# Gate and up pairs in seven products: two of the four weight sums made by adding DMAs, with signs turned

## The chip, the core and the metric

The kernel runs on one core of one Trainium2 chip, alone. The metric is the time of one execution on the device in microseconds (us). The core has five engines with queues of their own: TensorE (PE in the profile, its weight loads PEld), VectorE (DVE), ScalarE (ACT), GpSimd (POOL) and SyncE (SP). Each works through its instructions in order and waits on semaphores. 16 DMA engines move data between device memory and SBUF; a transfer is begun by a queue of SyncE, ScalarE or GpSimd.

## The reference

One layer of a hybrid decoder: a SwiGLU network, a mixer (gated linear attention beside stick-breaking attention), and a second SwiGLU network, each with RMS norms around it. The change is in the gate and up products of both networks:

```python
def swiglu(x, w_gate, w_up, w_down):
    return (jax.nn.silu(x @ w_gate) * (x @ w_up)) @ w_down

h = x + 0.5 * rms_norm(swiglu(rms_norm(x, ffn1_pre_g), ffn1_w_gate, ffn1_w_up, ffn1_w_down), ffn1_post_g)
# ... the mixer ...
y = h + 0.5 * rms_norm(swiglu(rms_norm(h, ffn2_pre_g), ffn2_w_gate, ffn2_w_up, ffn2_w_down), ffn2_post_g)
```

The model width is 1024, the hidden width 2816 (22 tiles of 128), all in float32. There are 512 prompt tokens, 32 sample tokens and 16 meta tokens: 560 columns in the first network, 544 in the second.

## The kernel before

A float32 product is made of three matmuls: each operand is split into a high part, its rounding to fp32r (`hi`, made by ScalarE), and a low part, the rest (`lo`, made by VectorE), and high times high, low times high and high times low are added up in PSUM.

**Tiles R and S.** Of the 22 hidden tiles of a network, 0 to 2 are computed early by halves of the columns, 3 to 5 (R in `PLAN1` and `PLAN2`) in the plain way, and 6 to 21 (S) in seven products: 16 pairs in each network, 32 in all. A pair is gate and up of one tile. Its activations are taken as a 2 x 2 matrix of quarters (halves of the columns by halves of the 1024 inputs), its weights too (halves of the inputs by gate and up). Seven products of quarters or of sums of quarters, 4 k-steps of 3 matmuls each (`seven`, matmuls in lines 1266 to 1268), give the four output quarters after a few additions. That is 84 matmuls of 280 or 272 columns.

**The weight sums.** A weight quarter is 512 x 128, in SBUF 128 x 512. `Chunks.fetch` loads a pair with two calls, each into one `raw` tile of 128 x 1024 by two DMAs on SyncE's queue (line 638): r1 holds b11 (gate, upper half of the inputs) and b12 (up, upper half), r2 holds b22 (up, lower half) and b21 (gate, lower half). `weight_sums` (line 988) makes four differences on VectorE, each a tensor_tensor of 128 x 512 by the helper `tt` (line 166):

```python
t3 = b22 - b12      # into a tile t
t1 = b12 - b11      # in place, over b12 in r1
t2 = b22 - t1       # into the tile t
t4 = b21 - t2       # into a tile t4
```

`parts_of` then splits r1 (called b1), t, r2 (b2) and t4 into high and low parts (`parted`, line 977, and `parted_lo`). The low part of b1 and of b2 frees the raw tile, and the same step calls `fetch` for the next load. There are three raw tiles, so b2 of a pair frees the tile for r1 of the pair after next.

**The order.** The order on TensorE, VectorE, ScalarE and GpSimd is that in which the code issues it: `step()` is called after every 6 matmuls of a pair, and `weights_at` hangs work on these steps, counted from the pair's first matmul: the four sums at -10, -10, -9 and -8, b1 at -6 and -5 (high part, low part), t at -2 and -1, b2 at 0 and 1, t4 at 4 and 6. A pair has 14 steps. SyncE's queue is ordered by a scheduler.

**The activation sums** (`summed`, line 1134) are made once for each network, four for each of two pairs of k-tiles, by `tt`. **The outputs** are put together on VectorE from PSUM (`add`, `c22`, `c21` and a sum for c12 in `seven`).

**Space.** Nearly all else lies in one arena of SBUF. `PLACES` is a table of bytes that says for each `take` where its tile is put (names room...). An instruction that writes into a place waits for the last readers of what was there.

The down projections and the mixer's gates use `weight_sums` and `parts_of` too.

Of the kernel before, what the change touches and what calls it, by code (L numbers as in the profile page):

```python
# [9 lines left out]
F32 = mybir.dt.float32  # L10
# [4 lines left out]
ALU = mybir.AluOpType  # L15

P = 128
D = 1024
KD = D // P
# [30 lines left out]


PLACES = bytes.fromhex("""
0c060018121e242a7094908082848668766a5066565e5c787c5452724e7a5836221c884c8c6c3064484a6e60613a2e8a3e446236923c465a3036
281674404260917e91588e124e328c341e726c307e4a4c188a486e3e24647a882c3c38360c06625a6a42749244402a3a2e0c00605e5c1e201254
147c16220664465283006268826980660b50560660680a69866467808400620b660a0c2661066460676686186300606266671004650662646766
86286100646066671a10620660878663660c1c00621d8786640e2506662486871c60910064688786241a690666688687820a6800246564697662
6806666991008264690078680607082491770776681c069186424e3e343a74546e7266323c00368c4468767c2840781e6c820c0238708c762a2e
26927c8a040660622a2c4816246527702e1262186071152c622a2b2d6415712c1262632a622a2b2d642c71626306180c1e62714b71246a003254
883e64604b38020434308a6058763c786222122a482e4c4a8e2c7b84668c687e7f406056464f3d333579036b366e747044426c7215015939318b
7782893f055514157a804e5a7e825c2483284e655e92647c508d3a521e148c822667648466616764656766422c7016604668746c6e647244206a  # L60
0a6612088a6c1804343c8c780688916a761a720f026e22320e1c103057565584641486544000760c676a6c8a7248082e604c1a3e582a910e2c66
301c856e001257421002685655542040164675150c8a146a0a300e121e188c782a2c007074107620060421863442736c6e728988846475668e0c
17343e12324c4a42460b7476486a3c1c3004436e20080972621a3736876660860a436c8417686e8e6a642c1488568c430408063c906394708417
6664606c6e78728e8a68846a86606e17708468646a6c7894728e668a0c866e606c176478686a848e728a66706e6c866072177084026836646a6c
8e00786686948a6e401c6620721a1e178a646030948e106c0c6a0e181c2068708486366e786a4072102a221e20170094667038840e1a6e8e0c1c
60724068641c8a1e1a186c220260206e8e59540e2a0c84721e302e68100066606c94641e3840202200706694308e8464606e4740721002682e0e
6c6630002a6884548c880c1456648e6e701660946c586e0c040e463c144754621206329074442e087674582c0a6c160c40102e2c006611466e43
705658544472340862403010322a1200024406343090916e0a436d0610160c72620840909066466c726c625670540a58406e084672020e540a6e
44163c4000100c064614404372561213020410703c3d423e000e4c6e161246483c060444420b1048704c0a023e494072006e480e14166e424412
463c560a2a7460309461704c8c8d2e904a4862766660346c6d670e88303276406c8c6663629500102c623e8876947254586667000e0a01006667  # L70
00105466403e88560d0c7273000c068a508e86202264366a1e7c7880268492524e34603a141a7e487a68734246824a733c3e58901b1717722e38
6e174c2840245a17175c7074442a5e5d1876668c54509212583e903c12151556622c88526c1b484a464215687f7b7e7a151b683a4e601b6a845c
1b18678d8053932d3078156577556381891c2282516d57648a5e1272384c2e1e828e906e868418403e36582416749432426a340c00605a5c484a
30683c44463a0c4e62702a56882c121e922022066416547f00607a7e7b80660b768c0662640a650c6c677e7800640e66060a600f06620e67660c
7a1000641166670e0419066218676610801800641966671a0c1906621c181d660a1b0064241a251c18630666266227241a65001c286429261067
06244e664f280e5000261d1c064e62520624292800501c4f00264e080928062524020308006c14862c486672504c8e4e1268926052880208047a
64304a2e3c82600a5884220c0280566a622410460e1e360842000a060418200302060e10030211060c0d0504020c110304020e1005030c181e30
24363d3440243a3e243865268202906c626e70
""")


class Arena:
# [52 lines left out]
def hybrid_step(  # L135
# [16 lines left out]
    take, give = arena.take, arena.give  # L152
# [6 lines left out]
    count = [0]  # L159
# [5 lines left out]
    def tt(out, a, b, op, eng=None):  # L165
        (eng or V).tensor_tensor(out=out, in0=a, in1=b, op=op)  # L166

    def stt(out, a, s, b, op0, op1):
        V.scalar_tensor_tensor(out=out, in0=a, scalar=s, in1=b, op0=op0, op1=op1)  # L169
# [454 lines left out]
    class Chunks:  # L624
# [5 lines left out]
        def fetch(self):  # L630
            if self.todo:
                w, r0, kt, c0, nw, kept = self.todo.pop(0)
                if kept == "quarters":

                    count[0] += 1
                    raw = sp.tile([P, kt, nw], F32, tag="raw", name=f"raw{count[0]}")
                    for i, w_ in enumerate(w):
                        nc.sync.dma_start(raw[:, 4 * i : 4 * i + 4],
                                          w_[r0 : r0 + 4 * P, c0 : c0 + nw].rearrange("(k p) n -> p k n", p=P))
# [323 lines left out]
    def gate_up_weights(plan, g_, u_, f0):  # L963
        for f in range(f0, KF):
            if f < RE_FFN or plan[f - RE_FFN] == "R":
                st.todo.extend((w, 0, KD, P * f, P, f < RE_FFN and "tile") for w in (g_, u_))
            else:
                st.todo.extend((w, r0, KD, P * f, P, "quarters") for w, r0 in (((g_, u_), 0), ((u_, g_), 4 * P)))

    quarters = {}  # L970

    def parted(f, key, src, room=None):

# [14 lines left out]
    def weight_sums(f, n):  # L988

        if n == 0:  # L990
            quarters[f] = st.raws.pop(0)[0], st.raws.pop(0)[0], take(KD * P), take(4 * P)
        r1, r2, t, t4 = quarters[f]
        t, t4 = (x.rearrange("p (k n) -> p k n", n=P) for x in (t, t4))
        b11, t1, b22, b21, t2, t3 = r1[:, :4], r1[:, 4:], r2[:, :4], r2[:, 4:], t[:, :4], t[:, 4:]
        tt(*((t3, b22, t1), (t1, t1, b11), (t2, b22, t1), (t4, b21, t2))[n], ALU.subtract)

    def parts_of(f, key):
        r1, r2, t, t4 = quarters[f]
# [95 lines left out]
    def other_tiles(old, gain, rs, nw, wid, hid, pairs, plan, late, sums_at, begun):  # L1094
# [5 lines left out]
        QW = nw // 2  # L1100
        QS = (slice(0, QW), slice(QW, nw))
# [4 lines left out]
        start_, n = {}, 0  # L1106
# [27 lines left out]
        def summed(i, n):  # L1134

            x, y = (pairs_of(pr_[j]) for j in (i, i + 2))
            if n == 0:
                for m in range(2):
                    sr_[i, m] = take(2 * NT)
            (s1, s2), (s3, s4) = ([pairs_of(sr_[i, m])[:, :, c] for c in QS] for m in range(2))  # L1140
            a11, a21, a12, a22 = x[:, :, QS[0]], x[:, :, QS[1]], y[:, :, QS[0]], y[:, :, QS[1]]
            tt(*((s1, a21, a22, ALU.add), (s3, a11, a21, ALU.subtract), (s2, s1, a11, ALU.subtract), (s4, a12, s2, ALU.subtract))[n])

        def sums_hi(i, m):
            for k in range(2):
# [75 lines left out]
        def seven(f):  # L1221
# [3 lines left out]
            o = {}  # L1225
# [16 lines left out]

            def c22():
                o["up"], o["sl"] = take(NT), take(NT)
                tt(o["up"][:, QS[1]], o["u2"][:, :QW], o["v"][:, :QW], ALU.add)
                give(o["v"])

            def c21():
# [1501 lines left out]
```

## Time and profile before

| | us |
|---|---|
| three runs | 1492.54, 1493.01, 1493.69 |
| median | 1493.01 |
| span of the profiled execution | 1491.2 |
| TensorE busy in it | 1482.6 |
| VectorE busy | 1106.0 |
| ScalarE busy | 783.1 |
| GpSimd busy | 68.4 |
| packets of queue q1 (SyncE), share of the 16 DMA engines | 44.7% |

The profile is of one execution on the chip. L12 is line 12 of the kernel; most of VectorE's instructions stand at the lines of two helpers, 166 (`tt`) and 169 (`stt`). A row of a group reads: line, engine, operation, output <- inputs by the program's names, sizes in partitions x elements, count | busy us, mean ns of one | idle time of the engine before them and what ended it. A row of the timeline begins with its start and its length in us. SPq is SyncE's queue of DMAs.

### The profile page before, as it was taken

To read this page: it belongs to the slowest core of one execution; us is meant where nothing else is said; L and a number is where in the kernel's file an instruction comes from. 1 tells how busy PE (TensorE), PEld (TensorE's weight loads), DVE (VectorE), ACT (ScalarE), POOL (GpSimd) and SP (SyncE) were. 2 spreads that over 40 slices of the span, in tenths; PEclk is the share of its full clock that TensorE was granted. 3 is DMA by queue.
4 is the path that set the end of the run, shared out by engine and by line. 5 is a ranking of instruction groups with operands and counts; after the bars stand their busy time and mean duration, and the time that the engine had idled before them with its cause. 6 is when DMAs were issued, how large, how long until landed. Compare 5 with 4: busy or idle time off the path is not lost.

```text
span 1491.2 us, 29865 instructions
## 1 busy us (share of the span) xinstructions
PE 1482.6 (99%) x11909; PEld 1435.2 (96%) x11909; DVE 1106.0 (74%) x1945; ACT 783.1 (53%) x1453; POOL 68.4 (5%) x145
## 2 busy tenths in 40 slices
PE   9999999999999999999999999999999999999998
PEld 8999999999999899999998999999999999999998
DVE  5888888855677866877887845777567898888544
ACT  7455454533555656566666543634564455455333
POOL 2000000000000011112111000000000000000000
PEclk9999999999999999999999999999999999999999
DMA  8133333324665584336555866344531333333253
GB/s 253 50 92 100 100 96 92 97 79 123 172 153 138 148 151 100 86 95 161 125 112 160 228 162 200 96 110 140 155 111 52 100 100 100 99 107 92 79 152 115
DMA packets 277230, 181.97 MB, mean 122 GB/s; under 512 B 10429, under 2 KB 255363, under 8 KB 277091
## 3 DMA queue, kind: packets, MB, share of 16 engines
q1 hardware_dynamic: 276786, 180.00, 44.7%
q8 instruction: 93, 1.52, 0.4%
q14 instruction: 47, 0.38, 0.1%
q0 software_dynamic: 288, 0.07, 0.0%
q10 hardware_dynamic: 16, 0.00, 0.0%
HBM read 155.06 MB, written 24.97 MB: 121 GB/s over the span
## 4 chain that ended last, share of the span: by engine, by line
PE 96%; DVE 2%; ACT 1%; DMA 1%; issue 0%; DVEq 0%; ACTq 0%
PE acc L1266 8%; PE acc L1267 8%; PE acc L1268 8%; PE acc L699 7%; PE acc L700 7%; PE acc L702 7%; PE acc L712 6%; PE acc L715 6%; PE acc L713 6%; PE acc L1046 2%; PE acc L1047 2%; PE acc L1048 2%; PE acc L1209 2%; PE acc L1206 2%; PE acc L1207 2%; PE ps L2041 1%
## 5 line engine op out<-in xcount | busy, mean ns | idle before, releaser
L166 DVE TENSOR_TENSOR room<-room,room 128x544 f32<-128x544 f32 (+18 forms) x457 | 285.6, 648 | 72.3 <-ACT room L779 16.7
L166 DVE TENSOR_TENSOR lo<-raw,hi 128x1024 fp32r<-128x1024 f32 (+1 forms) x207 | 248.1, 1199 | 105.5 <-ACT hi L678 66.7
L1266 PE MATMUL acc<-room,hi 128*128 128x280 f32 (+1 forms) x896 | 260.0, 290 | 0.0
L1268 PE MATMUL acc<-room,lo 128*128 128x280 f32 (+1 forms) x896 | 259.6, 290 | 0.0
L1267 PE MATMUL acc<-room,hi 128*128 128x280 f32 (+1 forms) x896 | 259.4, 289 | 0.0
L699 PE MATMUL acc<-room,hi 128*128 128x280 f32 x832 | 241.1, 307 | 0.2 <-DVE room L169 0.2
L700 PE MATMUL acc<-room,hi 128*128 128x280 f32 x832 | 225.0, 289 | 0.0
L977 ACT CAST hi<-raw 128x1024 fp32r<-128x1024 f32 x100 | 104.8, 1052 | 146.2 <-PE acc L1267 48.6
L702 PE MATMUL acc<-room,lo 128*128 128x280 f32 x832 | 173.1, 289 | 0.0
L1267 PEld LDWEIGHTS acc<-room,hi 128*128 128x128 f32 x896 | 168.9, 188 | 0.0
L1266 PEld LDWEIGHTS acc<-room,hi 128*128 128x128 f32 x896 | 168.8, 188 | 0.0
L1268 PEld LDWEIGHTS acc<-room,lo 128*128 128x128 f32 x896 | 168.6, 188 | 0.0
L699 PEld LDWEIGHTS acc<-room,hi 128*128 128x128 f32 x832 | 156.8, 188 | 10.1 <-issue 8.1
L700 PEld LDWEIGHTS acc<-room,hi 128*128 128x128 f32 x832 | 157.2, 189 | 1.2
L678 ACT CAST hi<-raw 128x1024 fp32r<-128x1024 f32 (+1 forms) x107 | 108.2, 1013 | 75.2 <-issue 21.5
L702 PEld LDWEIGHTS acc<-room,lo 128*128 128x128 f32 x832 | 130.3, 189 | 0.0
L977 ACT CAST hi<-room 128x1024 fp32r<-128x1024 f32 x92 | 76.9, 836 | 87.3 <-PE acc L1267 58.5
L166 DVE TENSOR_TENSOR lo<-room,hi 128x1024 fp32r<-128x1024 f32 x92 | 87.9, 955 | 43.4 <-ACT hi L977 43.0
L712 PE MATMUL acc<-room,hi 128*128 128x280 f32 (+2 forms) x388 | 110.8, 295 | 0.0
L713 PE MATMUL acc<-room,hi 128*128 128x280 f32 (+2 forms) x388 | 108.9, 290 | 0.0
L166 DVE TENSOR_TENSOR room<-room,acc 128x272 f32<-128x272 f32 (+1 forms) x180 | 76.2, 437 | 43.8 <-PE acc L1048 20.9
L712 PE MATMUL acc<-room,room 128*128 128x280 f32 (+3 forms) x364 | 107.4, 295 | 0.0
(397 smaller groups left out, 3437.2 us busy)
## 6 DMA issues: line engine op xcount, KB each, us to landing
raw<-in_w_in_dram SPq DMA_DIRECT2D x43, 512.0 KB, 7.2
raw<-in_ffn_w_gate_dram SPq DMA_DIRECT2D x64, 256.0 KB, 3.1
raw<-in_ffn_w_up_dram SPq DMA_DIRECT2D x64, 256.0 KB, 3.4
raw<-in_ffn_w_down_dram SPq DMA_DIRECT2D x36, 448.0 KB, 3.9
raw<-in_w_in_dram SPq DMA_DIRECT2D x40, 256.0 KB, 4.7
out_dram<-room SPq DMA_DIRECT2D x36, 256.0 KB, 3.7
room<-in_cache_k_dram SPq DMA_DIRECT2D x32, 256.0 KB, 5.7
room<-in_cache_v_dram SPq DMA_DIRECT2D x32, 256.0 KB, 4.7
```

The lines of the kernel that those rows point to most:

```text
L166: (eng or V).tensor_tensor(out=out, in0=a, in1=b, op=op)
L678: S.copy(h_, src)
L699: T.matmul(acc[h][:, : wid[h]], hi[k], a[h][0], start=(k == order[0]), stop=False)
L700: T.matmul(acc[h][:, : wid[h]], hi[k], a[h][1], start=False, stop=False)
L702: T.matmul(acc[h][:, : wid[h]], lo[k], a[h][0], start=False, stop=(k == order[-1]))
L712: T.matmul(acc[h][:nw, : wid[h]], wh, a[h][0], start=(k == 0), stop=False)
L713: T.matmul(acc[h][:nw, : wid[h]], wh, a[h][1], start=False, stop=False)
L715: T.matmul(acc[h][:nw, : wid[h]], wl, a[h][0], start=False, stop=(k == kt - 1))
L977: S.copy(hi[:, :kt], src)
L1266: T.matmul(x[:, :QW], hi, act[k][0], start=(first and k == 0), stop=False, skip_group_check=True)
L1267: T.matmul(x[:, :QW], hi, act[k][1], start=False, stop=False, skip_group_check=True)
L1268: T.matmul(x[:, :QW], lo, act[k][0], start=False, stop=(k == 3), skip_group_check=True)
```

## The change

For the 32 pairs, and for them alone, `fetch` has a new kind, "adding". For r1 it loads b11 and b12 as before, and then GpSimd begins a third DMA that adds b11 onto b12 in SBUF, so that t1 is made there. For r2 it loads b22 and b21, takes the tile t at once, loads b22 into t's second half as well, and GpSimd begins a DMA that adds b12 onto it: t3. `weight_sums` skips its first two steps for such pairs, and its last two are additions. To make all four weight sums additions, signs are turned elsewhere: of the activation sums, one (s1) becomes a subtraction and two (s2, s4) become scalar_tensor_tensor, (in0 x -1) - in1, and so do the sums of c22 and c12. An adding DMA waits for the landing of what it adds to, on GpSimd's queue. The tile t is held from the fetch on, and `PLACES` is another table.

```diff
-0c060018121e242a7094908082848668766a5066565e5c787c5452724e7a5836221c884c8c6c3064484a6e60613a2e8a3e446236923c465a3036
+12481e0c1a262a5b52840b8264048e7e6c7c00807a9042606a687062320294068810307292443c8a6e76860a2f8c74365658544e38783a66064e
...
             if self.todo:
                 w, r0, kt, c0, nw, kept = self.todo.pop(0)
+                if kept == "adding":
+
+                    count[0] += 1
+                    raw = sp.tile([P, kt, nw], F32, tag="raw", name=f"raw{count[0]}")
+                    x, y = (w_[r0 : r0 + 4 * P, c0 : c0 + nw].rearrange("(k p) n -> p k n", p=P) for w_ in w)
+                    nc.sync.dma_start(raw[:, :4], x)
+                    nc.sync.dma_start(raw[:, 4:], y)
+                    room = None
+                    if r0 == 0:
+                        nc.gpsimd.dma_start(raw[:, 4:], x, accum_op=ALU.add)
+                    else:
+                        room = take(KD * P)
+                        t3 = room.rearrange("p (k n) -> p k n", n=P)[:, 4:]
+                        nc.sync.dma_start(t3, x)
+                        nc.gpsimd.dma_start(t3, w[0][: 4 * P, c0 : c0 + nw].rearrange("(k p) n -> p k n", p=P), accum_op=ALU.add)
+                    self.raws.append((raw, room, kept))
+                    return
                 if kept == "quarters":
...
-                st.todo.extend((w, r0, KD, P * f, P, "quarters") for w, r0 in (((g_, u_), 0), ((u_, g_), 4 * P)))
+                st.todo.extend((w, r0, KD, P * f, P, "adding") for w, r0 in (((g_, u_), 0), ((u_, g_), 4 * P)))
...
         if n == 0:
-            quarters[f] = st.raws.pop(0)[0], st.raws.pop(0)[0], take(KD * P), take(4 * P)
+            (r1, _, kept), (r2, t, _) = st.raws.pop(0), st.raws.pop(0)
+            quarters[f] = r1, r2, take(KD * P) if t is None else t, take(4 * P)
+            adding[f] = kept == "adding"
+        if adding[f] and n < 2:
+            return
...
-        tt(*((t3, b22, t1), (t1, t1, b11), (t2, b22, t1), (t4, b21, t2))[n], ALU.subtract)
+        tt(*((t3, b22, t1), (t1, t1, b11), (t2, b22, t1), (t4, b21, t2))[n], ALU.add if adding[f] else ALU.subtract)
...
-            tt(*((s1, a21, a22, ALU.add), (s3, a11, a21, ALU.subtract), (s2, s1, a11, ALU.subtract), (s4, a12, s2, ALU.subtract))[n])
+            if n < 2:
+                tt(*((s1, a22, a21, ALU.subtract), (s3, a11, a21, ALU.subtract))[n])
+            else:
+                stt(*((s2, s1, -1.0, a11, ALU.mult, ALU.subtract), (s4, s2, -1.0, a12, ALU.mult, ALU.subtract))[n - 2])
...
-                tt(o["up"][:, QS[1]], o["u2"][:, :QW], o["v"][:, :QW], ALU.add)
+                stt(o["up"][:, QS[1]], o["u2"][:, :QW], -1.0, o["v"][:, :QW], ALU.mult, ALU.subtract)
...
-                         (13, lambda: tt(o["up"][:, QS[0]], o["u2"][:, :QW], d[:, :QW], ALU.add)), (15, c21),
+                         (13, lambda: stt(o["up"][:, QS[0]], o["u2"][:, :QW], -1.0, d[:, :QW], ALU.mult, ALU.subtract)), (15, c21),
```

On VectorE, at the weight sums of one pair in the middle of the first network's pairs (raw137 is its r1, raw140 its r2, room6_2_67 its t), there stands before:

```order
L166 TENSOR_TENSOR room6_2_67<-raw140_1996,raw137_1927 128x512
L166 TENSOR_TENSOR raw137_1927<-raw137_1927 128x512
L166 TENSOR_TENSOR room6_2_67<-raw140_1996,raw137_1927 128x512
L166 TENSOR_TENSOR lo148_2076<-room100_47_743,hi148_2075 128x512
L166 TENSOR_TENSOR room96_51_1019<-raw140_1996,room6_2_67 128x512
L166 TENSOR_TENSOR room134_58_1381<-room98_50_886,acc145_2041 128x280
L166 TENSOR_TENSOR room98_50_886<-room134_58_1381,acc146_2042 128x280
L166 TENSOR_TENSOR lo149_2110<-raw137_1927,hi149_2109 128x1024
```

and now, with room6_11_119 as its t:

```order
L166 TENSOR_TENSOR room6_11_119<-raw140_2007,raw137_1939 128x512
L166 TENSOR_TENSOR lo148_2090<-room124_60_1262,hi148_2089 128x512
L166 TENSOR_TENSOR room30_3_68<-raw140_2007,room6_11_119 128x512
L166 TENSOR_TENSOR room30_3_68<-room6_11_119,acc145_2054 128x280
L166 TENSOR_TENSOR room30_3_68<-room36_6_71,acc146_2055 128x280
L166 TENSOR_TENSOR lo149_2122<-raw137_1939,hi149_2121 128x1024
```

The first two rows of before, t3 and t1, are gone; t2 is the first, and the rest follows as it did.

On SyncE's queue, the loads of the same pair and its neighbours before:

```order
L638 DMA raw130_1872<-in_ffn1_w_up_dram 128x4x128
L638 DMA raw130_1872<-in_ffn1_w_gate_dram 128x4x128
L638 DMA raw137_1927<-in_ffn1_w_gate_dram 128x4x128
L638 DMA raw137_1927<-in_ffn1_w_up_dram 128x4x128
L638 DMA raw140_1996<-in_ffn1_w_up_dram 128x4x128
L638 DMA raw140_1996<-in_ffn1_w_gate_dram 128x4x128
```

and now:

```order
L646 DMA room78_9_89<-in_ffn1_w_up_dram 128x4x128
L638 DMA raw130_1882<-in_ffn1_w_up_dram 128x4x128
L639 DMA raw130_1882<-in_ffn1_w_gate_dram 128x4x128
L638 DMA raw137_1939<-in_ffn1_w_gate_dram 128x4x128
L639 DMA raw137_1939<-in_ffn1_w_up_dram 128x4x128
L646 DMA room36_6_71<-in_ffn1_w_up_dram 128x4x128
L638 DMA raw140_2007<-in_ffn1_w_up_dram 128x4x128
L639 DMA raw140_2007<-in_ffn1_w_gate_dram 128x4x128
```

The loads into raw tiles keep their order; the loads of b22 into a tile t (L646) stand between them, ahead of the pair that they belong to.

On GpSimd's queue, which had nothing to do in this stage, the adding DMAs of three of these pairs stand behind each other now, t1 (L642) and t3 (L647) of a pair in turn:

```order
L642 DMA raw127_1814<-in_ffn1_w_gate_dram 128x4x128
L647 DMA room54_51_870<-in_ffn1_w_up_dram 128x4x128
L642 DMA raw137_1939<-in_ffn1_w_gate_dram 128x4x128
L647 DMA room6_11_119<-in_ffn1_w_up_dram 128x4x128
L642 DMA raw147_2064<-in_ffn1_w_gate_dram 128x4x128
L647 DMA room78_9_89<-in_ffn1_w_up_dram 128x4x128
```

The instructions of TensorE and ScalarE stand in the order of before; on GpSimd's queue some memsets in the mixer's start change places with each other and with three mask operations.

More of the change, by code (lines that the diff above doesn't have):

```diff
@@ L52 @@
 PLACES = bytes.fromhex("""
-0c060018121e242a7094908082848668766a5066565e5c787c5452724e7a5836221c884c8c6c3064484a6e60613a2e8a3e446236923c465a3036
-281674404260917e91588e124e328c341e726c307e4a4c188a486e3e24647a882c3c38360c06625a6a42749244402a3a2e0c00605e5c1e201254
-147c16220664465283006268826980660b50560660680a69866467808400620b660a0c2661066460676686186300606266671004650662646766
-86286100646066671a10620660878663660c1c00621d8786640e2506662486871c60910064688786241a690666688687820a6800246564697662
@@ L57 @@
[L57 to L76, printed above, removed]
@@ L77 @@
-64304a2e3c82600a5884220c0280566a622410460e1e360842000a060418200302060e10030211060c0d0504020c110304020e1005030c181e30
-24363d3440243a3e243865268202906c626e70
+12481e0c1a262a5b52840b8264048e7e6c7c00807a9042606a687062320294068810307292443c8a6e76860a2f8c74365658544e38783a66064e
+241834403e3c0a09069446262c5c2e2a4e5a5e620232440772920e301a768a6e86100c885438587874661214164a8c484c20543d1834007a8e90
+427e6860042426766a6d641f413854367c0970803e1b0a1a204e583d826c1824403c381e1c297c26361b0664564e2754551a2050584f18293f3e
@@ new lines @@
+37243c647c263b36071a40061e2920224e543e64386528182419367d3a291b7c20540664081e1f0a4e183865287d7c54241a3a64221e0a1f1808
+20654f55544e247c28641e510a6508221b1855192624542c2a647c603092863244528c7e8e664e1e427a72160890685a501a0c1c188854562e26
+123c583e4048141e721636282d0608072612881e042425261613148873241512278972141289738872151417160c125a4a1e7372492d44583b3a
+8a3c8820213e7866627040287e686a823832342002041e52002248721836942706601c92804f8b83413d7f69468c761a4248545608636b594579
+718626293f672f07278e2d646c4e244c317a7c30906e2e884a0a748608502f72362d064e313095942e0a2d808c181c761a304860922a94062e5e
@@ new lines @@
+5a225c821612100c34570e32143a59667e782c0a68706a55928a623c6160293e404244262a54944693028220765e1612224e1a50662c2b628a7f
+70307e68803c788c045c3e7961600218085a0a2a1e2e5946821c9492622c3032208a42485444762b68800f143c8c290c107026713404027f0057
+7e52551e2e404e542a0368821a78946008060e1c9281445e465a3b3a298c76700a45145080168438127e3e0c660f6a5794003c18602622340807
+8a781c92465a046230483a427650702d2b5c7e80095e8c122014168438048a92074332706276224678441c8c301450125a2b067e20163834802c
+5c84080a04623a78461470768a92505f448c1c223248425a2c08125c0a808438303a3462787e067614200416462b92504280708a2c0a5e5c5a08
@@ new lines @@
+1244628c38323022764820041c068446442b165e1412388a082c5c0a5a2250062070928c8004628444425c467050061c088a2b22045a2c0a5e92
+16125c14203870440c8a6a6650100e421c920a081666506a6002475e3c464268002e571e943e182a0682666a92162c221c052528422004149459
+5a12186650522a5c3e686a1c44465000571e2e42940504222a59932c1c5c3e6a52142016926804125a666a162e2a1822521e5800041250205c3e
+165a5e2c2e601e022a3c005718521c1d1460122c04055e2e4e501a16405e3e5a1c2a125456042e056002155a2c141a1c18165c564e500052403e
+3c0416146660545c025525462f2e9294426a828a69445e6806070855285a2d685c182c54072f08161a1c8202545715208a062f072d0a2c080968
@@ new lines @@
+1406221e68022082082c8a8b062a0c3612147a167e787c728c303a90868e8038626e6c7648335e88686471243c46447594403e66030261425284
+70926a4e8a7400340232502692604c4b4836125918825c3540663e56330203542880385a1a9588643c2494684546444700036c5e626e04947632
+8603699190683b3a727c20835b39553758481e01815d13198e1c327a8616144a788c527e4270206a8a4e7602006092745084943d077c64667288
+2e566c6e2c2a0c253c10181a584412824a54464c1e38809024625b403401685e7d08063d5c3c000c202841480a2225372638105a6234697d6802
+5e3f7c32411e3625203c24223e631f0e383a7d5d627c5f01680c0534365c4124201e63287d3e000e68225f32627c05365d2041247d633e012634
@@ L79 @@
+00280562695c100e687c413e6336242600320569045c011003286863627c24413e38393632040068027c6214764e6c508a4a8228784c84748c16
+7a5a726a42889454706e582e86123c403e362c2a0c841e7454340e8610248c2f2e0c32861075852a748784110c3285118684751087745a361e0e
+4574290c448d8486462428196c007632268c42
 """)
@@ L967, in gate_up_weights @@
             else:
-                st.todo.extend((w, r0, KD, P * f, P, "quarters") for w, r0 in (((g_, u_), 0), ((u_, g_), 4 * P)))
-    quarters = {}
+                st.todo.extend((w, r0, KD, P * f, P, "adding") for w, r0 in (((g_, u_), 0), ((u_, g_), 4 * P)))
+    quarters, adding = {}, {}
     def parted(f, key, src, room=None):
```

## The prediction

> **What bounds the kernel now.** I read the page's first part, then the busy times by stretch, and then one pair in the timeline.
>
> ```profile
> span 1491.2 us, 29865 instructions
> PE 1482.6 (99%) x11909; PEld 1435.2 (96%) x11909; DVE 1106.0 (74%) x1945; ACT 783.1 (53%) x1453; POOL 68.4 (5%) x145
> ```
>
> TensorE is idle for 1491.2 - 1482.6 = 8.6 us in the whole span. A busy TensorE need not be one at its best pace, since the ends of matmuls are modelled, so the number of matmuls in a stretch says more. In these rows the columns are the stretch, its length, busy us and count of PE, PEld, DVE, ACT and POOL, the granted clock, the share of the DMA engines, and GB/s.
>
> ```profile
> 0.00:75.00 75.00, 73.20 (x529) 69.20 (x530) 54.06 (x115) 44.97 (x97) 8.96 (x25) 1.00 0.52 153
> 150.00:225.00 75.00, 75.00 (x585) 75.00 (x584) 64.54 (x98) 36.83 (x56) 0.00 (x0) 1.00 0.34 99
> 300.00:375.00 75.00, 75.00 (x585) 75.00 (x585) 37.50 (x55) 26.64 (x44) 0.00 (x0) 1.00 0.36 109
> 1200.00:1275.00 75.00, 75.00 (x600) 75.00 (x600) 66.29 (x100) 38.18 (x59) 0.00 (x0) 1.00 0.36 105
> 1350.00:1425.00 75.00, 75.00 (x600) 75.00 (x600) 53.47 (x86) 33.03 (x55) 0.00 (x0) 1.00 0.34 97
> 1425.00:1491.20 66.20, 60.62 (x486) 59.45 (x484) 29.46 (x45) 26.27 (x46) 0.00 (x0) 0.99 0.41 127
> ```
>
> The second row is pairs of the first FFN, the third the matmuls of its down projection. VectorE works 64.54 us in one and 37.50 in the other, and TensorE issues 585 matmuls in both, one every 75/585 = 0.128 us. The second FFN (600 and 600, with 66.29 and 53.47 us of VectorE) says the same. So in the pairs, where alone the change takes work away, TensorE already runs at the pace that it has when VectorE is half idle. The clock is granted in full. Of the 8.6 us of idle time, 1.8 lie in the first row and 5.6 in the last, the kernel's start and its last tiles; 1.2 us are left for all between.
>
> **The change, part by part.**
>
> *VectorE.* The sums t3 and t1 of 32 pairs go, 64 instructions of the first two kinds below. 72 tensor_tensor become scalar_tensor_tensor: 8 activation sums of 560 columns and 64 output sums of 280.
>
> ```profile
> L166 DVE TENSOR_TENSOR room<-raw,raw 128x512 f32<-128x512 f32 x92 | 63.4, 689 | 5.9 <-DMA raw<-in_ffn_w_down_dram 3.1 <-DMA room<-in_cache_k_dram 1.1 <-DMA raw<-in_w_in_dram 0.2
> L166 DVE TENSOR_TENSOR raw<-raw 128x512 f32<-128x512 f32 x46 | 31.8, 692 | 1.6
> L166 DVE TENSOR_TENSOR room<-room,room 128x560 f32<-128x560 f32 x44 | 32.2, 737 | 4.2 <-ACT room L1090 2.6 <-ACT room L1065 1.2
> L169 DVE SCALAR_TENSOR_TENSOR room<-room,room 128x560 f32<-128x560 f32 x4 | 3.0, 740 | 2.1 <-ACT room L312 2.1
> L166 DVE TENSOR_TENSOR room<-room,acc 128x280 f32<-128x280 f32 x70 | 29.8, 442 | 11.7 <-PE acc L1268 10.1 <-PE acc L1432 1.4
> L169 DVE SCALAR_TENSOR_TENSOR room<-acc,room 128x280 f32<-128x280 f32 x4 | 1.8, 442 | 0.0
> ```
>
> The swaps cost 740 - 737 = 3 ns and 442 - 442 = 0 ns each: nothing. The removal takes 64 x 0.69 = 44 us of VectorE's 1106, all of it under a TensorE that does not wait for it. Worth on the path: 0.
>
> *TensorE and ScalarE* keep their instructions and their order; the 7 x 4 x 3 = 84 matmuls of a pair still take 84 x 0.128 = 10.8 us. Other places in SBUF change who waits for whose old tile. Set against the times of before, no wait between two engines in the new order asks for something that ends later than its reader began: worth 0, with a micro-wait of some tenths either way.
>
> *The transfers.* A pair had four loads of 256 KB; now it has five and two adding ones, so 32 x 3 x 0.256 MB = 25 MB more. SyncE issues 32 more DMAs, GpSimd 64. The question is whether the adding ones land in time. Here is one pair of the first FFN (start, length): VectorE's freeing of a buffer; SyncE's issues of its refill (gate, up) and of the next buffer; this pair's VectorE work, t3, t1 and t2 first; ScalarE's rounding of b1; TensorE's first matmuls with its high and its low part.
>
> ```profile
> 159.44 1.23 DVE L166 TENSOR_TENSOR lo<-raw,hi 128x1024 fp32r<-128x1024 f32 x1
> 160.69 0.37 SPq L638 DMA_DIRECT2D raw<-in_ffn_w_gate_dram  x1
> 161.11 0.50 SPq L638 DMA_DIRECT2D raw<-in_ffn_w_up_dram  x1
> 166.91 0.37 SPq L638 DMA_DIRECT2D raw<-in_ffn_w_up_dram  x1
> 172.04 0.69 DVE L166 TENSOR_TENSOR room<-raw,raw 128x512 f32<-128x512 f32 x1
> 172.76 0.69 DVE L166 TENSOR_TENSOR raw<-raw 128x512 f32<-128x512 f32 x1
> 173.48 0.69 DVE L166 TENSOR_TENSOR room<-raw,raw 128x512 f32<-128x512 f32 x1
> 174.09 0.68 DVE L166 TENSOR_TENSOR lo<-room,hi 128x512 fp32r<-128x512 f32 x1
> 174.70 0.69 DVE L166 TENSOR_TENSOR room<-raw,room 128x512 f32<-128x512 f32 x1
> 175.30 0.80 DVE L166 TENSOR_TENSOR room<-room,acc 128x280 f32<-128x280 f32 x2
> 176.46 1.23 DVE L166 TENSOR_TENSOR lo<-raw,hi 128x1024 fp32r<-128x1024 f32 x1 [0.36 <-ACT hi L977]
> 175.38 1.05 ACT L977 CAST hi<-raw 128x1024 fp32r<-128x1024 f32 x1 [2.17 <-DVE room L166]
> 179.90 0.29 PE L1266 MATMUL acc<-room,hi 128*128 128x280 f32 x1
> 180.15 0.29 PE L1268 MATMUL acc<-room,lo 128*128 128x280 f32 x1
> ```
>
> And the durations from issue to landing, with what GpSimd's issue of 128 rows takes (587 ns):
>
> ```profile
> raw<-in_ffn_w_gate_dram SPq DMA_DIRECT2D x64, 256.0 KB, 3.1
> raw<-in_ffn_w_up_dram SPq DMA_DIRECT2D x64, 256.0 KB, 3.4
> raw<-in_ffn_w_gate_dram SPq DMA_DIRECT2D x11, 512.0 KB, 4.0
> room<-in_state_gla_dram SPq DMA_DIRECT2D x16, 256.0 KB, 7.2
> sbb<-in_sb_bias_dram POOLq DMA_DIRECT2D x1, 8.0 KB, 5.2
> L217 POOL DMA_DIRECT2D sbb<-in_sb_bias_dram x1 | 0.6, 587 | 0.0
> ```
>
> The refill is issued until 161.11 and lands at 161.11 + 3.4 = 164.5; there GpSimd, idle in this stage, can begin the add of t1, and 0.6 later that of t3. The first reader of t1 is t2, at 173.48: **9.0 us** without any delay of VectorE. TensorE can stand more. After t1's landing VectorE does t2, the low part of t4, t4, the two sums (0.61 + 0.61 + 0.60 + 0.80) and b1's low part (1.23), together 3.85 us, which must end by 180.15: landing by 176.3, that is **11.8 us** after GpSimd's start. t3 has longer, since ScalarE rounds the t tile only after b1.
>
> No row shows an adding DMA. From below it is a plain gate load, 3.1. From above it is the 128-row transfer of GpSimd's queue, 5.2, and on top the slowest landing of 256 KB, 7.2: 12.4. Between them: 5.2 for a nearly empty transfer, and data time. 256 KB more cost 4.0 - 3.1 = 0.9 us; an add reads what it adds and what it adds to, so I take 1.8; and t1 and t3 of a pair run side by side, so 3.6: **8.8 us**, nearest to the GpSimd row, and inside 9.0. The plain loads of t2's other operand are issued at 166.91 and have 173.48 - 166.91 = 6.6 us against 3.4, and 9.4 until TensorE would notice. So nothing is late: cost 0.
>
> On the DMA engines, four loads a pair fill 0.34 of the time. With an add at two loads it becomes 0.34 x (5 + 2 x 2)/4 = 0.77; at one load, 0.34 x 7/4 = 0.60. Both leave room.
>
> [...]
>
> *New waits.* VectorE's t2 and ScalarE's rounding of b1 now wait for a GpSimd transfer. Behind t2 on VectorE are the low part of t4 and the sums that read TensorE's accumulators; behind b1 on ScalarE the Silu of c11. SyncE's refill of a buffer waits for the add in it; the add ends before VectorE's last reading, so this wait is met already. On SyncE's queue t3's load stands between the refills at 0.4 to 0.5 us an issue. Cover for all this is the 11.8 us; without it every missing us counts.
>
> **Sum.** 0 on the path. The profiled execution spans 1491.2 us, 1.8 less than the median of the runs, 1493.01; unchanged means 1493.0, with 1 us or so for micro-waits. A difference under 0.2%, 3 us, is not told from none.
>
> **Rivals.**
>
> *A late add (slower).* If an add takes more than 11.8 us from GpSimd's start, TensorE waits in every pair. A buffer filled for pair n+2 is freed by pair n, so the loss per two pairs is the excess: 16 x (X - 11.8). At the upper bound 12.4 that is 10 us: 1503. For it: no adding DMA in the trace, and landings of 7.2 us exist. Against: it needs three times the data time that I took.
>
> *Full DMA engines (slower).* 0.34 x (5 + 2k)/4 passes 1 at k = 3.4 loads for an add. At k = 4 it is 1.10, a pair takes 11.9 instead of 10.8 us, and 32 pairs cost 36 us: 1529. Against: the second read accounts for k = 2 only.
>
> *GpSimd held up by VectorE (slower).* VectorE's row for two pairs leaves little room:
>
> ```profile
> 150.00:171.60 21.60, 21.60 (x170) 21.60 (x169) 18.61 (x29) 10.61 (x16) 0.00 (x0) 1.00 0.34 98
> ```
>
> 3.0 us are idle there, in pieces of some 0.4 to 0.6 us, as long as one issue (587 ns). If GpSimd could build a transfer only in such pieces, an add might start as late as VectorE's longest stretch in the rows above, from 172.04 to 176.1 without a pause, 4 us: 8.8 + 4 = 12.8, 1.0 too late, 16 x 1.0 = 16 us, 1509. [...]
>
> *VectorE's relief pays (faster).* TensorE has eight waits that VectorE ends, 1.1 to 0.2 us, together 3.5:
>
> ```profile
> PE acc L1493 <- DVE own L270: 1.1, 1, 1.1
> PE acc L715 <- DVE lo L166: 0.6, 1, 0.6
> ...
> PE ps L873 <- DVE room L166: 0.2, 1, 0.2
> ```
>
> If all of them went, 1493.0 - 3.5 = 1489.5. Against: none of them is in a pair (their lines are the start's, the plain products' and the last tiles'), and the pace is the same at half of VectorE's load.
>
> **How the numbers follow.** Unchanged 0.75; late add 0.12; full engines 0.06; GpSimd held up 0.03; relief 0.04. So faster 0.04, same 0.75, slower 0.21. The range goes from 1489.5 (relief) to 1503 (the upper bound of the add); full engines and a held-up GpSimd, 0.09, and what a late add could do beyond, stay outside. Without the rivals it would be 1491.5 to 1495.
>
> **What would show it.** Right: 585 and 600 matmuls in the stretches of pairs, VectorE near 1062 us, GpSimd's 64 issues near 0.6 to 0.8 us, their landing under 11.8 us, a DMA share of 0.6 to 0.8 in the pairs, and no PE wait that goes back to a weight tile. Wrong: TensorE's waits in the pairs' matmuls for a low part whose VectorE instruction stood behind a DMA of GpSimd (late add); a share of 0.95 or more with plain loads landing late too (full engines); long spans of GpSimd's issues (held up).

## The result, and the profile after

The changed kernel takes 1496.75 us (median of 13 runs), the kernel before 1493.30 in 13 runs beside them: a ratio of 1.0022, 95% interval 1.0014 to 1.0030. That is slower by 3.45 us, little more than the 0.2% that was called the bound of what can be told, and the interval excludes no change. Forecast was no change, at 0.75.

The profiled execution of the changed kernel took 1495.3 us, of which 1493.6 are its span. Its first rows:

```profile
span 1493.6 us, 30078 instructions
PE 1483.9 (99%) x11909; PEld 1436.4 (96%) x11909; DVE 1066.9 (71%) x1881; ACT 783.4 (52%) x1453; POOL 150.3 (10%) x209
```

The stretches of before, again with length, busy us and count of PE, PEld, DVE, ACT and POOL, clock, DMA share and GB/s:

```profile
150.00:225.00 75.00, 75.00 (x582) 75.00 (x581) 55.55 (x83) 36.22 (x56) 18.03 (x14) 1.00 0.81 167
300.00:375.00 75.00, 75.00 (x585) 75.00 (x584) 37.80 (x58) 26.47 (x44) 0.67 (x3) 1.00 0.36 106
375.00:450.00 75.00, 73.81 (x557) 68.99 (x556) 55.08 (x89) 44.61 (x89) 0.57 (x3) 1.00 0.63 160
1200.00:1275.00 75.00, 75.00 (x599) 75.00 (x598) 57.21 (x88) 37.45 (x59) 18.02 (x14) 1.00 0.85 176
```

VectorE lost 9 us of 75 in the pairs, GpSimd gained 18, the DMA share went from 0.34 to 0.81. TensorE issues 582 matmuls from 150 to 225 us where it issued 585, 599 from 1200 where it issued 600, and from 375 to 450 us it is busy for 73.81 us where it was 74.40, in this row of before:

```profile
375.00:450.00 75.00, 74.40 (x563) 69.80 (x563) 55.27 (x92) 46.12 (x93) 1.24 (x6) 1.00 0.62 157
```

That stretch is not one of pairs: there the down projection of the first network ends and the mixer begins. TensorE's list of waits has one entry that was not there before, and one that was 0.6:

```profile
PE acc L732 <- DVE lo L166: 0.7, 1, 0.7
PE acc L729 <- ACT hi L695: 0.4, 1, 0.4
```

The transfers of the pairs (KB each, median us from issue to landing):

```profile
raw<-in_ffn_w_gate_dram SPq DMA_DIRECT2D x64, 256.0 KB, 4.4
raw<-in_ffn_w_up_dram SPq DMA_DIRECT2D x64, 256.0 KB, 4.1
...
room<-in_ffn_w_up_dram SPq DMA_DIRECT2D x32, 256.0 KB, 5.0
raw<-in_ffn_w_gate_dram POOLq DMA_DIRECT2D x32, 256.0 KB, 5.4
...
room<-in_ffn_w_up_dram POOLq DMA_DIRECT2D x32, 256.0 KB, 7.2
```

The add for t1 lands after 5.4 us, the one for t3 after 7.2. No add is late for TensorE.

Both programs issue the same 11909 matmuls in the same order, so the start of each can be set against that of the same matmul before. What a stretch adds to the difference from the first profile of before, in us, with how much more time passes from the last matmul's start to the end of the span (tail):

| profile | 0 to 45 | first network's pairs, 84 to 258 | boundary, 354 to 395 | 950 to 1045 | tail |
|---|---|---|---|---|---|
| before, a second one | 0.25 | 0.00 | 0.07 | 0.00 | 0.40 |
| before, a third one | -0.06 | 0.00 | 0.23 | 0.00 | 0.00 |
| the change | 0.65 | 0.93 | 0.79 | -0.40 | 0.37 |
| the change, a second one | 0.02 | 0.93 | 2.16 | -0.40 | 0.93 |
| the change, a third one | 0.26 | 0.93 | 2.80 | -0.40 | 0.62 |

All stretches left out add up to 0.1 us or less in each row, but for 0.3 after 1045 us in the last row: among them are the pairs of the second network, with as many adding DMAs as those of the first. So the spans of the last three rows are 2.4, 3.6 and 4.5 us longer than that of before. Three terms belong to the change: a steady 0.93 us in the first network's pairs, 0.40 us given back in the mixer, and 0.8 to 2.8 us at one boundary.

### The boundary at 376 us

Here the mixer's first weights are loaded (`fetch_early`, 512 KB of `w_in`, line 651 before, 668 after; these are columns of the values, though some of the expectations below call them gate weights), the last down weights too (line 199), and the rows of x that are added at the end (line 1312, now 1336). SyncE's queue before and after, from the traces (start, length from the first issue to the end of the last, number):

```profile
362.52 1.33 SPq L1312 DMA_DIRECT2D room<-h_dram  x3
365.20 0.38 SPq L199 DMA_DIRECT2D raw<-in_ffn_w_down_dram  x1
365.63 0.58 SPq L651 DMA_DIRECT2D room<-in_w_in_dram  x1
368.29 4.35 SPq L199 DMA_DIRECT2D raw<-in_ffn_w_down_dram  x3
```

```profile
360.49 4.45 SPq L1336 DMA_DIRECT2D room<-h_dram  x3
364.98 0.43 SPq L668 DMA_DIRECT2D room<-in_w_in_dram  x1
366.81 0.38 SPq L199 DMA_DIRECT2D raw<-in_ffn_w_down_dram  x1
367.23 0.58 SPq L1336 DMA_DIRECT2D room<-h_dram  x1
369.84 2.99 SPq L199 DMA_DIRECT2D raw<-in_ffn_w_down_dram  x2
```

The single load of line 199 in the middle is issued 1.6 us later than before, and TensorE's matmuls are 1.6 us later here too. But the mixer's load, which stood behind it, now goes first. ScalarE rounds what the load of line 199 brings (128 x 1024) as soon as it is there, before and after:

```profile
369.82 1.05 ACT L678 CAST hi<-raw 128x1024 fp32r<-128x1024 f32 x1 [1.43 <-DMA raw<-in_ffn_w_down_dram]
```

```profile
374.76 1.05 ACT L695 CAST hi<-raw 128x1024 fp32r<-128x1024 f32 x1 [4.82 <-DMA raw<-in_ffn_w_down_dram]
```

It was there 369.82 - 365.20 = 4.6 us after its issue, and now 374.76 - 366.81 = 8.0 us. TensorE waits for it, and then for the low part that VectorE makes from it:

```profile
375.86 0.40 PE L729 MATMUL acc<-room,hi 128*128 128x280 f32 x1 [0.45 <-ACT hi L695]
377.12 0.40 PE L732 MATMUL acc<-room,lo 128*128 128x280 f32 x1 [0.74 <-DVE lo L166]
```

That the load is late because 512 KB stand ahead of it was a reading of one trace. So was that the order came from the table of places and not from the transfers in the pairs. The experiments test both.

### The profile page after: what moved, and what is told of

It reads as the page before. It is cut to its first block, busy times and chain, and to the rows that moved or that the text cites. A ratio compares the mean times of both kernels' runs of the same rounds, so it can differ in the third digit from the quotient of the medians.

```text
span 1493.6 us, 30078 instructions
## 1 busy us (share of the span) xinstructions
PE 1483.9 (99%) x11909; PEld 1436.4 (96%) x11909; DVE 1066.9 (71%) x1881; ACT 783.4 (52%) x1453; POOL 150.3 (10%) x209
## 3 DMA queue, kind: packets, MB, share of 16 engines
q0 software_dynamic: 34080, 16.85, 9.1%
## 4 chain that ended last, share of the span: by engine, by line
PE 96%; DVE 2%; ACT 1%; DMA 1%; issue 0%; DVEq 0%; ACTq 0%; SPq 0%
PE acc L1290 8%; PE acc L1291 8%; PE acc L1292 8%; PE acc L716 7%; PE acc L717 7%; PE acc L719 7%; PE acc L729 6%; PE acc L732 6%; PE acc L730 6%; PE acc L1067 2%; PE acc L1068 2%; PE acc L1069 2%; PE acc L1230 2%; PE acc L1233 2%; PE acc L1231 2%; PE ps L2065 1%
## 5 line engine op out<-in xcount | busy, mean ns | idle before, releaser
L166 DVE TENSOR_TENSOR room<-room,room 128x544 fp32r<-128x544 f32 (+16 forms) x437 | 271.7, 643 | 72.8 <-ACT room L796 17.8
L729 PE MATMUL acc<-room,room 128*128 128x280 f32 (+3 forms) x362 | 106.7, 295 | 0.0
L730 PE MATMUL acc<-room,room 128*128 128x280 f32 (+3 forms) x364 | 105.3, 289 | 0.0
```

What stands on the lines that cost most here:

```text
L729: T.matmul(acc[h][:nw, : wid[h]], wh, a[h][0], start=(k == 0), stop=False)
L730: T.matmul(acc[h][:nw, : wid[h]], wh, a[h][1], start=False, stop=False)
```

## The experiments

In the first four runs theory A says that the added transfers cost the time by their bytes, A2 that the adding does, B that the places and signs do, C that VectorE's relief gains and the transfers lose more.

**The changed kernel without transfers.** The output stays.

```diff
-                    if r0 == 0:
-                        nc.gpsimd.dma_start(raw[:, 4:], x, accum_op=ALU.add)
-                    else:
+                    if r0:
                         room = take(KD * P)
-                        t3 = room.rearrange("p (k n) -> p k n", n=P)[:, 4:]
-                        nc.sync.dma_start(t3, x)
-                        nc.gpsimd.dma_start(t3, w[0][: 4 * P, c0 : c0 + nw].rearrange("(k p) n -> p k n", p=P), accum_op=ALU.add)
...
-        if adding[f] and n < 2:
-            return
```

> The changed kernel without its adding DMAs and without the third load of a pair: four loads as before, t3 = b22 + b12 and t1 = b12 + b11 made on VectorE again. The signs, the table of places and the early take of t stay. The change measured +3.3 us, a ratio of 1.0022. Theory A (the added transfers cost it): nearly all of it goes, ratio to the kernel before 1.0000 to 1.0006, DMA share in the stretch 150 to 225 us back at 0.34 and 585 matmuls there. Theory B (the new places and signs cost it): it stays, ratio 1.0018 to 1.0026, with the wait at the boundary to the down projection (0.4 and 0.7 us at the lines of the plain products). Theory C (VectorE's relief gains some and the transfers cost more): above 1.0000 by less than A says, at most 1.0003.

Measured: 1496.22 us, ratio 1.0019 (1.0010 to 1.0028). VectorE and the DMA engines are back where they were, the matmuls are not, and the new wait is longer:

```profile
150.00:225.00 75.00, 75.00 (x582) 75.00 (x581) 64.18 (x97) 36.20 (x56) 0.00 (x0) 1.00 0.34 98
```

```profile
PE acc L724 <- ACT hi L690: 1.4, 1, 1.4
...
PE acc L727 <- DVE lo L166: 0.7, 1, 0.7
```

This kernel has none of the added transfers, and its loss is that of the change within the intervals (1.0019 and 1.0022). A, A2 and C fall; B stands.

**Without the adds alone, with plain DMAs in their place, and with a wider load.**

```diff
-                        nc.gpsimd.dma_start(raw[:, 4:], x, accum_op=ALU.add)
-                        nc.gpsimd.dma_start(t3, w[0][: 4 * P, c0 : c0 + nw].rearrange("(k p) n -> p k n", p=P), accum_op=ALU.add)
```

> The changed kernel without the 64 adding DMAs, and with nothing in their place, so that t3 is b22 and t1 is b12 (the output is another one). Five plain loads a pair and VectorE relieved of 64 sums. Theory A (the bytes of the transfers cost it, whatever makes them): 1 of 3 added transfers is left, ratio 1.0004 to 1.0010. Theory A2 (it is the adding ones, by their reading and writing in SBUF or by GpSimd's issues): 1.0000 to 1.0004. Theory B (places and signs): 1.0018 to 1.0026.

```diff
-                        nc.gpsimd.dma_start(raw[:, 4:], x, accum_op=ALU.add)
+                        nc.gpsimd.dma_start(raw[:, 4:], x)
...
-                        nc.gpsimd.dma_start(t3, w[0][: 4 * P, c0 : c0 + nw].rearrange("(k p) n -> p k n", p=P), accum_op=ALU.add)
+                        nc.gpsimd.dma_start(t3, w[0][: 4 * P, c0 : c0 + nw].rearrange("(k p) n -> p k n", p=P))
```

> The changed kernel with the 64 adding DMAs turned into plain ones of the same size from the same queue to the same place (t1 becomes b11 and t3 becomes b12, so the output is another one). Every instruction and its order stay. Theory A (bytes and GpSimd's issues): as the change, 1.0018 to 1.0026, with GpSimd's 150 us busy unchanged. Theory A2 (the adding itself): 1.0000 to 1.0010, DMA share in 150 to 225 us falls from 0.81 to about 0.60. Theory B (places and signs): 1.0018 to 1.0026 too; run e1 tells B from A.

```diff
-                        nc.sync.dma_start(t3, x)
+                        nc.sync.dma_start(room.rearrange("p (k n) -> p k n", n=P), w[0][:, c0 : c0 + nw].rearrange("(k p) n -> p k n", p=P))
```

> The changed kernel with the load of b22 into the tile t doubled: 512 KB fill all of t, of which the first half is not needed (t2 is written over it). One quarter more per pair, 8 MB in all; the output stays. Theory A (bytes): the loss grows by a third to a half, ratio 1.0027 to 1.0034. Theory A2 (the adding itself): as the change, 1.0018 to 1.0027. Theory B (places and signs): as the change. If the DMA engines come near to full (a share of 0.9 and over in the stretch from 150 to 225 us), adds can land late and the ratio is over 1.004.

Measured: 1498.34 us, 1.0028 (1.0016 to 1.0040, six runs) without the adds; 1497.67, 1.0020 (1.0011 to 1.0029) with plain DMAs; 1498.78, 1.0034 (1.0021 to 1.0048, five runs) with the wider load. (The ratios are taken from all runs, not from the medians. The runs with plain DMAs fall into two groups, five of 1495.07 to 1496.45 us and six of 1497.67 to 1497.96, and the six are those with a mean granted clock of 0.998.) The pairs of the first network give 0.93 us and the mixer -0.40 in all three, as in the change and in the run without transfers. The boundary gives 3.26, 1.04 and 3.09. Fewer transfers gain nothing, as B says (the first and the last are above its numbers, and both their profiles have a wait of 1.4 us at the boundary, and the halved clock after it that is told below). The 1.0034 of the wider load is also what theory A gave for it, so that number alone does not decide; the run without the adds does, since it has less to transfer and loses no less. The wider load's extra, 1.5 us in its profile, has a place of its own in the second network, at the DMA share of its row there; the second and third fence are TensorE's wait and VectorE's sum t2:

```profile
1200.00:1275.00 75.00, 75.00 (x600) 75.00 (x599) 53.70 (x82) 36.92 (x57) 18.02 (x14) 1.00 0.94 204
```

```profile
1277.80 0.39 PE L1290 MATMUL acc<-room,hi 128*128 128x272 f32 x1 [1.19 <-DVE room L166]
```

```profile
1275.15 0.69 DVE L166 TENSOR_TENSOR room<-raw,raw 128x512 f32<-128x512 f32 x1 [4.71 <-DMA raw<-in_ffn_w_gate_dram]
```

That is the rival of the late add, in one pair of 32 and at a share of 0.94: t2 waits 4.7 us for the add in its raw tile, and TensorE 1.2 us for t2. At 0.85, in the change, it doesn't happen, nor at 0.90, in the pairs of the first network with the wider load. The stretches of the other two kernels say what an add takes of the DMA engines:

```profile
150.00:225.00 75.00, 75.00 (x582) 75.00 (x581) 55.77 (x84) 36.24 (x55) 0.00 (x0) 1.00 0.42 120
```

```profile
150.00:225.00 75.00, 75.00 (x582) 75.00 (x581) 55.76 (x83) 36.20 (x56) 10.40 (x14) 1.00 0.59 166
```

Five loads a pair fill 0.42, so a plain load 0.084; two more from GpSimd (0.59 - 0.42)/2 = 0.085 each; two adds (0.81 - 0.42)/2 = 0.195 each, 2.3 plain loads.

In the next four runs theory A is the boundary: the new places let the mixer's load of `w_in` go first. Theory B is that the loss lies in the pairs and at the start.

**The mixer's load handed to SyncE later**, its tile taken as before: by 4 steps in the changed kernel, by 32 in it, and by 32 in the kernel before.

```diff
             self.early[r0, c0] = room = take(8 * P)
-            nc.sync.dma_start(room.rearrange("p (k n) -> p k n", n=2 * P),
-                              win[r0 : r0 + 4 * P, c0 : c0 + 2 * P].rearrange("(k p) n -> p k n", p=P))
+            later(4, lambda: nc.sync.dma_start(room.rearrange("p (k n) -> p k n", n=2 * P),
+                              win[r0 : r0 + 4 * P, c0 : c0 + 2 * P].rearrange("(k p) n -> p k n", p=P)))
```

> The changed kernel with one DMA issued later: the early load of the mixer's gate weights (512 KB, line 668 of the changed kernel) is handed to SyncE four steps after its tile is taken, so that it stands behind the load of the down weights that it stood ahead of, as in the kernel before. Nothing else is changed. Theory A (the new places let this load go first, the down weights land late, TensorE waits at 376 us and its clock drops for 3.4 us): the wait for ScalarE's high part at the plain products (0.45 us in the profile of the change, 1.4 in three of the experiments) is gone, no run shows the halved clock at 378 us, ratio to the kernel before 1.0002 to 1.0010. Theory B (the loss is in the pairs and at the start, 0.95 and up to 0.6 us, and the wait only moves a later one): 1.0016 to 1.0026.

> The same with 32 steps, so that this load stands behind five loads of the down weights. Theory A: the down weights land earlier than in the kernel before, the wait for VectorE's low part (0.6 us before, 0.74 in the change) goes too, ratio 0.9998 to 1.0006. Theory B: as the change, 1.0016 to 1.0026.

> The kernel before with the same delay of 32 steps for its early load of the gate weights. Theory A: its own wait of 0.6 us at 377.8 us goes, ratio 0.9994 to 0.9999. Theory B, or if the loads of the residual rows crowd the down weights instead: 0.9998 to 1.0004.

Measured: 1494.21 us, 1.0003 (0.9994 to 1.0012); 1493.74, 1.0000 (0.9991 to 1.0009); 1492.51, 0.9990 (0.9981 to 0.9999). With 4 steps SyncE's queue has the order of before at this place, and the wait for ScalarE's high part is gone from the list; with 32 both waits are. The first fence is the queue with 4 steps, the second TensorE with 32 from 370 to 390 us, where the kernel before has the third:

```profile
367.03 0.38 SPq L199 DMA_DIRECT2D raw<-in_ffn_w_down_dram  x1
367.45 0.58 SPq L668 DMA_DIRECT2D room<-in_w_in_dram  x1
370.05 4.34 SPq L199 DMA_DIRECT2D raw<-in_ffn_w_down_dram  x3
```

```profile
370.00:390.00 20.00, 20.00 (x154) 19.82 (x153) 7.45 (x8) 8.42 (x13) 0.00 (x0) 1.00 0.64 199
```

```profile
370.00:390.00 20.00, 19.40 (x147) 18.99 (x146) 6.98 (x8) 8.62 (x14) 0.00 (x0) 1.00 0.69 204
```

One DMA moved, and most of the loss is gone, with all adds in place: theory A. The boundary gives 0.12 us with 4 steps and -0.94 with 32; in the kernel before with 32 it gives -0.91. That last kernel is 0.1% below the kernel before, a little more than was expected, and has nothing of the change in it. With the delay of 32 in both, the changed kernel still takes 1493.74 - 1492.51 = 1.2 us more: the boundary is not all of the loss.

**The kernel before with the new places alone**: the table and the early take of t, with every sum on VectorE and with the old signs. The diff against the kernel before is the table, and in `fetch`:

```diff
+                    raw = sp.tile([P, kt, nw], F32, tag="raw", name=f"raw{count[0]}")
+                    x, y = (w_[r0 : r0 + 4 * P, c0 : c0 + nw].rearrange("(k p) n -> p k n", p=P) for w_ in w)
+                    nc.sync.dma_start(raw[:, :4], x)
+                    nc.sync.dma_start(raw[:, 4:], y)
+                    room = None
+                    if r0:
+                        room = take(KD * P)
+                    self.raws.append((raw, room, kept))
+                    return
```

> The kernel before with the new table of places and with the tile t taken at the fetch; no adding DMA, no third load, no sign turned: every sum as before. Theory A (places): 582 matmuls in the stretches 75 to 150 and 150 to 225 us, where the kernel before has 585, the wait and in some runs the halved clock at 376 us, ratio 1.0014 to 1.0026. If the turned signs cost the pace in the pairs: 585 matmuls, and a ratio lower by 0.0006. If neither: 1.0000.

Measured: 1496.53 us, 1.0021 (1.0012 to 1.0030), the whole loss. The pairs of the first network give 0.93 us, the mixer -0.40, the boundary 0.98:

```profile
150.00:225.00 75.00, 75.00 (x582) 75.00 (x582) 64.21 (x97) 36.19 (x56) 0.00 (x0) 1.00 0.33 97
```

Its queue at the boundary has the order of the change:

```profile
365.14 0.43 SPq L663 DMA_DIRECT2D room<-in_w_in_dram  x1
366.98 0.38 SPq L199 DMA_DIRECT2D raw<-in_ffn_w_down_dram  x1
```

So neither the signs nor the adds cost anything that can be measured. What costs is the new plan: where the tiles lie, and the order of SyncE's queue that comes with it.

**Both kernels again**, for what belongs to a single execution:

> The kernel before, once more, for a second profile. Two terms of the comparison may belong to the single execution and not to the change: the time up to which TensorE's clock is not granted in full at the start (4.5 us before, 6.0 in the change, 4.1 to 7.0 in the experiments) and the issue of one of the last stores on SyncE's queue (0.38 us before, 1.13 in the change, up to 2.1 in the experiments). If they are chance: this profile shows another start, and may show a longer issue at the end. If they are the change: 4.5 and 0.38 again. Either way 585 matmuls from 150 to 225 us and 0.6 us of wait at 377.8 us, with no halved clock.

> As the run before it: a third profile of the kernel before, same expectations.

> The changed kernel, once more. Theory A: 582 matmuls from 150 to 225 us again; the wait for ScalarE's high part at 376 us between 0.4 and 1.5 us; the time near 1495 to 1496 if it is short, and 1497 to 1498.5 with a halved clock at 377 us if it is 1.4. Rival: the times spread as much without it.

> As the run before it: a third profile of the changed kernel, same expectations.

Measured: before 1493.62 and 1493.12 us, the change 1496.55 and 1497.40; their rows stand in the table above. The start and the tail change from one execution to the next in the same kernel. In the tail, one of the last stores took 1.05 us to issue in one of the three profiles of before and 1.13 to 1.53 in all three of the change, where 0.38 is usual. Over all profiles an issue of more than 1 us is there in 8 of the 10 with the new places and in 1 of the 4 with the old ones, so part of the tail may belong to the change; why, stays open. The wait for ScalarE's high part was 1.8 and 0.9 us, the first longer than expected, and the halved clock came with the shorter one, which no theory had said. Its stretches:

```profile
374.00:377.40 3.40, 1.75 (x12) 1.30 (x11) 1.23 (x1) 1.27 (x2) 0.00 (x0) 1.00 1.01 276
377.40:380.90 3.50, 3.50 (x16) 3.50 (x17) 2.08 (x3) 2.34 (x4) 0.00 (x0) 0.51 0.81 236
380.90:384.00 3.10, 3.10 (x26) 3.10 (x25) 0.47 (x1) 0.00 (x0) 0.00 (x0) 1.00 1.00 304
```

and the second of them in the first profile of the change:

```profile
377.40:380.90 3.50, 3.50 (x29) 3.50 (x29) 2.17 (x3) 2.26 (x4) 0.00 (x0) 1.00 0.83 240
```

After 3.4 us in which TensorE was busy for 1.75, the granted clock is 0.51 for 3.5 us, with 16 matmuls where the other has 29. So the halved clock costs 13 matmuls of 0.13 us, 1.7 us, on top of the wait.

## Why the prediction was wrong

**The step that failed** is this one: "Other places in SBUF change who waits for whose old tile. Set against the times of before, no wait between two engines in the new order asks for something that ends later than its reader began: worth 0, with a micro-wait of some tenths either way." As far as it goes it may hold; it leaves out the order of SyncE's queue. The engines' order is written out by hand, SyncE's is made by a scheduler, and with the new table it put a 512 KB load ahead of a more urgent one, some 110 us behind the last pair of the first network. (That it did so because the load's place comes free earlier is argued, not shown.) The prediction looked at that queue only among the pairs. In place of "some tenths" the boundary measured 0.8, 2.2 and 2.8 us in three profiles. The same step took a matmul's pace to be the same at any place: in the first network's pairs it isn't, by 0.93 us, and -0.40 in the mixer. Sum: 0.93 - 0.40 = 0.5, and the boundary's 1.9 on average, of the 3.45 between the medians; start and tail (0.3 and 0.6 on average), which also differ within a kernel, are most of the rest. That 1496.75 lies between 1489.5 and 1503 is luck: the upper end was put there for a late add, and no add was late for TensorE.

**TensorE bounds, VectorE's relief is worth 0**: right. With the new places, without transfers and with VectorE at 64.18 us per stretch, TensorE has the 582 matmuls that it has with 55.55. The premise that 585 is its pace in any case was wrong by half a per cent.

**VectorE near 1062 us**: 1066.9, 39 us less and not 44. The two groups of sums lose what was forecast, 63.4 + 31.8 - 41.4 - 9.7 = 44.1, by these rows:

```profile
L166 DVE TENSOR_TENSOR room<-raw,raw 128x512 f32<-128x512 f32 x60 | 41.4, 690 | 21.1 <-DMA raw<-in_ffn_w_gate_dram 16.5 <-DMA raw<-in_ffn_w_down_dram 2.6 <-DMA raw<-in_w_in_dram 0.8
...
L166 DVE TENSOR_TENSOR raw<-raw 128x512 f32<-128x512 f32 x14 | 9.7, 692 | 0.5
```

But instructions of 0.69 us that follow each other begin 0.61 apart (the prediction's own timeline from 173.48 on), and busy time counts what overlaps once: the durations of all VectorE instructions add up to 44.1 us less, and their overlap falls from 98.0 to 92.9. The first row also shows what t2 waits for now: 16.5 us for transfers of gate weights, which are the adds of t1, all under TensorE's cover. The swapped instructions cost nothing, as forecast: with the old signs the loss is the same.

**The price of an add, 8.8 us within 3.1 to 12.4**: within the bounds, but too large. 5.4 us for t1 and 7.2 for t3, against 11.8 for which TensorE has cover. The 9.0 us up to t2 were too many. With t3 and t1 gone from VectorE, t2 comes earlier (it begins 0.65 us behind the sum of 128 x 560 ahead of it, 183.28 to 183.93, where before it was 2.10, 182.19 to 184.29), and the plain loads land later (4.4 and 4.1 us for 3.1 and 3.4): in the change, one pair behind the prediction's rows, these are the last plain load of a tile, the add onto it and its t2, 6.7 us behind the add's issue:

```profile
172.94 0.50 SPq L639 DMA_DIRECT2D raw<-in_ffn_w_up_dram  x1
177.20 1.27 POOL L642 DMA_DIRECT2D raw<-in_ffn_w_gate_dram  x1 [7.15 <-DVE room L166]
183.93 0.69 DVE L166 TENSOR_TENSOR room<-raw,raw 128x512 f32<-128x512 f32 x1
```

In 18 of the 32 pairs t2 waits for the add, 1.8 us at most (with plain DMAs in the place of the adds in none), and none of these waits reaches TensorE. The share of 0.77 was 0.81: an add counts for 2.3 plain loads and not for 2. That an add reads twice what a load reads, from which the prediction took its 1.8 us of data time and its two loads, was an assumption; no run shows what an add reads, only its 2.3 loads on the engines and its 5.4 and 7.2 us to landing. One size was off in the other way: GpSimd's issue of an add is 1.27 us for t1 and 1.82 for t3, not 0.6 to 0.8, and nothing waited for that. By line, in the change and then with plain DMAs:

```profile
L647 POOL DMA_DIRECT2D room<-in_ffn_w_up_dram x32 | 58.1, 1817 | 0.0
L642 POOL DMA_DIRECT2D raw<-in_ffn_w_gate_dram x32 | 40.6, 1270 | 593.2 <-DVE room L166 383.0 <-DVE room L169 93.1 <-DMA raw<-in_ffn_w_up_dram 59.8
```

```profile
L642 POOL DMA_DIRECT2D raw<-in_ffn_w_gate_dram x32 | 24.0, 750 | 623.3 <-DVE room L166 443.7 <-DMA raw<-in_ffn_w_up_dram 143.0 <-DMA room<-in_ffn_w_up_dram 27.2
```

**The rivals.** None of them is what happened. The late add exists, but was seen at a share of 0.94 alone. The DMA engines were not full in the pairs: their share is 0.81 and 0.85 in the change's rows above, and 0.90 and 0.94 with the wider load. GpSimd held up by VectorE: its issues are of even length (1256 to 1277 ns for t1 in the first network's pairs, but for the first with 1352), though VectorE is busy for as little as 0.35 and as much as 0.97 of one. In most of these pairs of before VectorE works with no pause over 0.04 us for 7.35 us (168.74 to 176.09 in one), and not for the 4 that the prediction read from fewer rows. VectorE's relief pays nothing. That something outside the pairs would become slower was no rival, and should have been one: the change brought a new table for all of the kernel.

## What to carry to other kernels

A new memory plan is a change of its own to all of the kernel, and every queue that a scheduler orders must be compared along its whole length, above all where stages meet and transfers crowd. When a small loss is found, run the kernel with the side effects of the change alone: here the table of places without its purpose had the whole loss. Work taken from an engine that nobody waits for bought nothing here: VectorE had 39 us less, and the ratio was 1.0022 where the new places alone gave 1.0021. A prefetch that stands ahead of an urgent load can be moved back for free: that gained 0.1% in the kernel before.

## What the runs showed of the hardware

**The clock was halved in four profiles of fourteen.** From 370 to 390 us the mean granted clock is 0.91 in the runs without transfers, without the adds and with the wider load, and in the third profile of the change; it is 1.00 in the other ten. In the stretch from 377.4 to 380.9 us it is 0.62, 0.55, 0.56 and 0.51 in those four. TensorE's two waits at the boundary add up to 2.1, 2.1, 2.1 and 1.6 us in them and to 1.4 us or less in nine of the others. In the second profile of the change they add up to 2.5 us (1.8 and 0.7), and the clock stayed at 1.00. So the length of the waits alone does not settle it; what else does was not tried.

**The pace of matmuls changed with where the tiles lie.** All ten profiles of kernels with the new places have 0.93 us more in the same 1350 matmuls, 0.7 ns each, at DMA shares from 0.33 to 0.90, and 582 matmuls from 150 to 225 us; the four profiles with the old places have 585 or 586 there and agree with each other to 0.01 us. Whether it is an operand's place, and which, was not tried.

**The adds went in smaller packets.** The software queue moved 16.85 MB in 34080 packets with adds, 494 bytes each on average, and in 5408 with plain DMAs of the same size, 3116 bytes each, on these rows of the change and of the kernel with plain DMAs:

```profile
q0 software_dynamic: 34080, 16.85, 9.1%
```

```profile
q0 software_dynamic: 5408, 16.85, 3.9%
```
